# A streaming encoder layer: weight pool switched behind the third sample group, the attention's first work cast ahead, its scores queued in front of the memory values

## The chip, the core and the metric

The kernel runs on one core of one Trainium2 chip. The metric is the device time of one execution in microseconds (us); the time before is the median of three runs. The engines are TensorE (PE, matrix products into PSUM; its weight loads are shown as PEld), VectorE (DVE), ScalarE (ACT), GpSimd (POOL) and SyncE (SP, which only issues DMAs here). Each engine runs its own queue in order and waits on semaphores. DMAs are issued from the queues of SP and ACT before the change, and from POOL's too behind it; all run on the same sixteen DMA engines.

## What is computed

One layer with 1024 prompt tokens and 64 sample tokens, so 1088 columns, of width 1024, in float32. The change touches the sliding-window attention (SWA), the retention branch's output product and the memory values:

```python
def swa_attend(q, k, v, bias, sinks, valid):
    s = jnp.einsum('bnqhgd,bnkhd->bnhgqk', q, k, preferred_element_type=jnp.float32) * (SWA_HD ** -0.5)
    s = s + bias.astype(jnp.float32)
    if valid is not None:
        s = jnp.where(valid, s, NEG_INF)
    sink = sinks.astype(jnp.float32)[:, :, None, None]
    m = jnp.maximum(jnp.max(s, axis=-1, keepdims=True), sink)
    e = jnp.exp(s - m)
    p = e / (jnp.sum(e, axis=-1, keepdims=True) + jnp.exp(sink - m))
    return jnp.einsum('bnhgqk,bnkhd->bnqhgd', p.astype(v.dtype), v)

def merge_branches(ret_o, ret_g, swa_o, gate_a, gate_b, w_ret_out, w_swa_out, w_mix_out):
    B, S = ret_g.shape[:2]
    a = (rms_norm(ret_o).astype(ret_g.dtype).reshape(B, S, -1) * jax.nn.silu(ret_g)) @ w_ret_out
    b = swa_o.reshape(B, S, -1) @ w_swa_out
    return (jax.nn.sigmoid(gate_a) * a + jax.nn.sigmoid(gate_b) * b) @ w_mix_out

def mem_kv(mem, g_mem, w_mk, w_mv):
    B = mem.shape[0]
    mn = rms_norm(mem, g_mem)
    return ((mn @ w_mk).reshape(B, N_MEM, MEM_HEADS, MEM_HD),
            (mn @ w_mv).reshape(B, N_MEM, MEM_HEADS, MEM_HD))
```
Queries come in 17 chunks of 64 tokens; a chunk sees its own and the two chunks before it, so 192 keys, except chunk 0 (64 keys) and chunk 1 (128). There are 16 query heads of width 64 on two key heads.

## The kernel before

**Products.** Large products are made from two float32r parts of each operand, a high part (a cast on ACT, line 123) and the rest (a subtraction on DVE, line 124): high times high, high times low, low times high (lines 149 to 151, and 205 to 208 inside Strassen's scheme). A projection of 256 output rows is one round of Strassen with seven products, P1, P2, P6, P5, P7, P3 and P4 in PE's order. Its seven weight operands lie in tiles `wq` (five of them in rotation, `self.wbufs`), made from two `raw` tiles by sums on POOL (lines 183 to 189) and the two-part split. The pool `weights` that holds `raw` and `wq` is opened with five `wq` for `project_phase` and again, at the same place, with six for all that follows.

**project_phase.** It runs k, q, v and the sample groups of the attention's queries (`w_sq`, four groups, 0 to 3) between the four heads of retention, then `w_sk`/`w_sv` and the third sample group, then twelve projections in three sets of four: `w_ga`, `w_rg`, `w_gb`. Each set's results go through a `stage` tile to DRAM as `d_gate[1]`, `[0]`, `[2]`; the sets `w_ga` and `w_gb` are stored from ACT's queue, `w_rg` from SP's. `memory_phase` is a generator whose parts are drawn between these projections by the list `steps`; it makes memory keys and the values of three of the four heads, from weights in three `mw` tiles.

**mix_phase.** `swa` holds the attention's loop, `filler` the products that are strewn between its steps. Work is cut into 34 halves (17 chunks, two halves of the query heads). At step i PE gets, in this written order (`in_order` ties each to the last matmul): `weigh` of half i-1, `scores` of half i+2, `turn` of half i (transposes of the normalised weights), and some filler pieces; steps -2 and -1 only make scores. A half's `scores` go into one PSUM tile `s` of two banks that exists once; DVE adds the bias (line 958 or 961), takes the maximum (963), compares with the sink (964), negates (965); ACT takes the exponential (970, 972); DVE makes the reciprocal (973, 974), POOL multiplies (976). `turn` transposes keys 0 to 127 into `pt0`, copied by ACT (993), and keys 128 to 191 into `pt1` with four 64-row pieces side by side in 512 columns, copied by DVE (995). `weigh` multiplies them with the value tiles (1006): one pair of matmuls for each part, one for each key head, which write rows 0 to 63 and 64 to 127 of one PSUM bank.

The fillers are, in order: the loading and splitting of all 24 pieces of the retention operand (`d_gate[0]`, three column chunks `CH` of 384, 384 and 320 for eight row blocks, into tiles `ret` of ring 1), the fourth head's memory values (four pieces), and the 24 products with `w_ret_out` (row block m by column chunk c, two pieces of 12 matmuls each). Four pieces come at step -2, forty over the 34 steps, eight at the end.

**What sets the order.** A planner orders every engine's queue by a simulated time line; `high_priority` moves work ahead in it, and `issue_after(ins)` ties what follows behind `ins` on the same engine's queue without a wait for its end. A tile waits until the last reader of what lay at its address is done. The SBUF rings 0 and 1 have eight slots each: during the projections ring 0 holds the operands B11, T1 and T4 and two slots of `stage`, ring 1 B21, B22, T2 and T3; afterwards ring 0 becomes the attention's `swin` tiles (keys, queries, bias, values, and ten small load buffers `lds`), ring 1 the `ret` tiles. PSUM has eight banks: three pairs (`psa`) and two single ones (`pr`) in the projections; then three for the plain products (`pd`) and five for the attention (`pw`).

Of the kernel before, what the change touches and what calls it, by code (L numbers as in the profile page):

```python
# [19 lines left out]
P = 128  # L20
# [9 lines left out]
H = 4  # L30
# [79 lines left out]
class Kernel:  # L110
# [222 lines left out]
    def run(self):  # L333
        nc, tc, io = self.nc, self.tc, self.io
        with ExitStack() as ctx:
# [34 lines left out]
            with ExitStack() as sctx:  # L370
                self.rings = [Ring(sctx.enter_context(tc.tile_pool(name=f"ring{i}", bufs=1, reuse_waits="tile", side="right")))
                              for i in range(2)]
                self.mem = sctx.enter_context(ExitStack())
                with self.weights(5):
                    self.project_phase()
                with self.weights(6):
                    with self.plain_psum():
                        self.mix_phase()
                        self.mem.close()
                        self.cross_phase()  # L380
                    rp = sctx.enter_context(tc.tile_pool(name="rf", bufs=1, reuse_waits="tile", side="right"))
                    self.rstd_f = rp.tile([P, T], F32, name="rstd_f")
                    self.temp = sctx.enter_context(ExitStack())
                    self.new_b12(self.temp, side="right")
                    self.cross_out_phase()
                    self.ffn_phase()

    @contextmanager
    def weights(self, bufs):
        self.wbufs = bufs  # L390
        with ExitStack() as ctx:
            self.wp = ctx.enter_context(self.tc.tile_pool(name="weights", bufs=2, reuse_waits="tile"))
            yield
# [88 lines left out]
    def memory_phase(self, mp):  # L482
# [8 lines left out]
        room = lambda: mp.tile([P, 1024], F32, tag="mw", bufs=3, name="mw")  # L491
# [21 lines left out]
        for h in range(H - 1):  # L513
            us = [self.unit(io["w_mv"][h, i], 4, 256, room) for i in range(2)]
            for t in range(2):
# [10 lines left out]
    def bias_table(self):  # L526
# [11 lines left out]
        row = self.np.tile([1, 16], F32, tag="row", bufs=1, name="row")  # L538
# [3 lines left out]
        for e in range(2):  # L542
            rows = slice(e * 64, (e + 1) * 64)
            nc.vector.tensor_copy(self.sinks[rows, :], ps[rows, :16].rearrange("p (a b) -> p a b", b=2)[:, :, e])

    def project_phase(self):
        nc, tc, io = self.nc, self.tc, self.io
        with ExitStack() as ctx:
            self.fp = ctx.enter_context(tc.tile_pool(name="fa", bufs=1, reuse_waits="tile"))
# [84 lines left out]
            with ExitStack() as rctx:  # L634
# [4 lines left out]
                for h in range(H):  # L639
# [20 lines left out]
            project(self.load_ops((io["w_sk"], io["w_sv"])), lambda i, t, o: self.store(self.d_skv[i, :, half(t)], o))  # L660
            project(pair("w_sq", 3), queries(3))
            steps = [0, 0, 0, 0, 1, 2, 2, 3, 3, 3, 2, 0]
            for idx, w, act in ((1, "w_ga", AF.Sigmoid), (0, "w_rg", AF.Silu), (2, "w_gb", AF.Sigmoid)):
                for m in range(0, KT, 2):
                    store = nc.scalar.dma_start if idx else self.store
                    put = lambda i, t, o, idx=idx, m=m, store=store: store(self.d_gate[idx][m + i, :, half(t)], o)
                    other = None if idx else lambda i, m=m: self.d_ret[m + i]
                    with tc.issue_after(project(pair(w, m // 2), put, act, other)):
                        for i in range(steps.pop(0)):
# [3 lines left out]
                            else:  # L673
                                next(memory)

# [209 lines left out]
    def swa(self, ctx, fill):  # L885
        nc, tc, io = self.nc, self.tc, self.io
        if True:
# [4 lines left out]
            flat = [t.rearrange("p a b -> p (a b)") for t in self.ring_tiles(0, KT, "swin", F32)]  # L892
            kT, vT = flat[0][:, :KC], flat[5][:, :KC]
            bias = flat[2][:, :NPAIR * NKEY].rearrange("p (a b) -> p a b", b=NKEY)
            sinks = self.sinks
            qTs = [t[:, :16 * 2 * 64].rearrange("p (i c e) -> p i c e", i=4, c=4) for t in (flat[1], flat[7])]
            vts = [flat[4][:, i * P:(i + 1) * P] for i in range(17)] + [flat[0][:, KC + i * P:KC + (i + 1) * P] for i in range(3)]
            self.lds = [t[:, i * 384:(i + 1) * 384] for t in (flat[3], flat[6]) for i in range(5)]
            with tc.high_priority():
                def tokens(dst, i, cache):  # L900
                    self.load(dst[:, :SEQ], self.d_skv[i, :, :SEQ])
                    self.load(dst[:, SEQ:SEQ + P], io[cache])
                    self.load(dst[:, SEQ + P:], self.d_skv[i, :, SEQ:])

                tokens(kT, 0, "ckT")
                self.load_queries(qTs, 0)
                raws = [self.unit_raw(io["w_mv"][H - 1, i], 4, 256) for i in range(2)]
                self.first_units = [self.unit_parts(raw, 4, 256) for raw in raws]
            with tc.high_priority(), tc.issue_after(self.loaded):
                for e in range(2):  # L910
                    src = self.d_rb.rearrange("(p e) c -> e c p", e=2)[e, 63:63 + 64 * 255, :]
                    src = src.rearrange("(i c) p -> i p c", c=255)[:, :, :NKEY]
                    self.load(bias[e * 64:(e + 1) * 64], src)
# [26 lines left out]
            def scores(c, hf):  # L940
                ks, j0, nk = keys(c)
                if hf == 0 and c % 4 == 0 and c + 4 < 17:
                    self.load_queries(qTs, c + 4)
# [20 lines left out]
                nc.vector.tensor_tensor(out=nm, in0=nm, in1=snk, op=ALU.max)  # L964
                nc.vector.tensor_scalar(nm, nm, -1.0, None, ALU.mult)
                den = sw.tile([P, 2, 2], F32, tag="den", name="den")
                es = sw.tile([P, 2, 2], F32, tag="es", name="es")
                nc.vector.tensor_tensor(out=es, in0=snk, in1=nm, op=ALU.add)
# [3 lines left out]
                nc.scalar.activation(es, es, AF.Exp)  # L972
# [7 lines left out]
            def turn(c, hf):  # L980
                ks, j0, nk = keys(c)
                if hf == 0:
                    live[c] = [values(ks + k0) for k0 in range(0, nk, P)]
                t, vt = live.pop((c, hf)), live[c]
                parts = []
                for k0 in range(0, nk, P):
                    n = min(P, nk - k0)
                    pp = pw.tile([P, 512], F32, tag=f"pt{len(parts)}", name="pp")
                    for j, (v, i) in enumerate(units):
                        self.last_mm = nc.tensor.transpose(pp[:n, j * P:(j + 1) * P], t[:, v, i, k0:k0 + n], self.ident).ins  # L990
                    pT = sw.tile([P, 512], F32, tag=f"pT{len(parts)}", bufs=2, name="pT")
                    if len(parts) == 0:
                        nc.scalar.copy(pT[:n, :], pp[:n, :])
                    else:
                        nc.vector.tensor_copy(pT[:n, :], pp[:n, :])
                    parts.append((vt[k0 // P], pT, n))
                live[c, hf] = parts

            def weigh(c, hf):
# [4 lines left out]
                for j, (val, pT, n) in enumerate(parts):  # L1004
                    for v in range(2):
                        self.last_mm = mm(po[rows[v], hf * 256:(hf + 1) * 256], val[:n, rows[v]], pT[:n, v * 256:(v + 1) * 256],  # L1006
                                          start=j == 0, stop=j == len(parts) - 1).ins
# [13 lines left out]
            for i in range(-2, n):  # L1021
# [8 lines left out]
                if i == -2:  # L1030
                    with tc.high_priority(), tc.issue_after(self.operand_loaded):
                        tokens(vT, 1, "cvT")
                if i == 8:
                    with tc.issue_after(self.loaded):
                        keep()
            self.in_order(lambda: weigh(*halves[n - 1]))
            for pieces in next(fill):
                self.in_order(lambda: next(pieces, None))

# [19 lines left out]
    def filler(self):  # L1059

        nc, tc, io = self.nc, self.tc, self.io
        if True:
            def ld():
                self.lds.append(self.lds.pop(0))
                return self.lds[-1]

# [636 lines left out]
```

## Time and profile before

| | |
|---|---|
| median of three runs | 2243.72 us (2242.51 to 2244.74) |
| profiled execution, its own time | 2244.47 us |
| profiled execution, span from first to last instruction | 2242.7 us |
| mean granted PE clock | 0.988 |
| PE busy in 0 to 480 us | 458.36 us |
| PE busy in 1015 to 2242.7 us | 1190.29 us of 1227.70 |

The profile is one execution. Engine times are busy times; a group of instructions is given by its line, engine, operation and tiles, with its count, busy time, mean duration in ns and the idle time of its engine just ahead of it and what ended that. In a table of windows each row is a stretch of the span, with each engine's busy time, PE's granted clock as a share of full speed, and the DMA engines' busy share. In a timeline a row is start, duration, engine and line, with the count of merged instructions and in brackets the idle time ahead and what released it. Matmuls overlap in PE's pipeline, so their durations add up to more than the time that they take.

### The profile page before, as it was taken

How to read it: one execution, taken by the hardware profiler on the slowest of the kernel's cores; microseconds unless marked ns; L12 is line 12 of the kernel's file. 1: busy time of each engine (PE TensorE's matmuls, PEld its weight loads, DVE VectorE, ACT ScalarE, POOL GpSimd, SP SyncE). 2: the span in 40 equal slices, each digit the busy share in tenths (PEclk: the TensorE clock that was granted, in tenths of full speed). 3: DMA queues.
4: the chain of work that ended last, by engine and by line, in shares of the span. 5: the costliest groups of instructions: out<-in, count | busy, mean ns of one | idle time of the engine just before them, and what ended most of it. 6: DMA issues, size and time to landing. Idle time of an engine off the chain costs nothing.

```text
span 2242.7 us, 41756 instructions
## 1 busy us (share of the span) xinstructions
PE 2168.9 (97%) x16434; PEld 2105.3 (94%) x16434; DVE 1596.0 (71%) x2655; ACT 885.4 (39%) x1897; POOL 692.1 (31%) x466
## 2 busy tenths in 40 slices
PE   8899999999999989999999999999999999999986
PEld 8899999999999977779999998999999999999986
DVE  7986878666687667776455556668777677778587
ACT  7333333435444355554133333333323222344243
POOL 1441533342253112220000000014556555434462
PEclk9999999999999999999999999999999999999998
DMA  5533445443445475326443111422333332475233
GB/s 193 163 108 114 118 124 136 133 126 114 167 151 181 150 229 163 114 69 211 132 152 101 64 46 59 138 89 88 121 129 102 102 120 90 147 267 184 85 98 108
DMA packets 182599, 290.86 MB, mean 130 GB/s; under 512 B 40290, under 2 KB 110850, under 8 KB 182402
## 3 DMA queue, kind: packets, MB, share of 16 engines
q1 hardware_dynamic: 177794, 279.26, 39.3%
q10 hardware_dynamic: 4608, 8.91, 1.1%
q8 instruction: 130, 2.13, 0.4%
q14 instruction: 67, 0.55, 0.1%
HBM read 196.95 MB, written 91.16 MB: 128 GB/s over the span
## 4 chain that ended last, share of the span: by engine, by line
PE 79%; DVE 11%; DMA 5%; issue 2%; ACT 2%; POOL 1%; SPq 0%; DVEq 0%; ACTq 0%; POOLq 0%
PE pq L208 15%; PE pq L206 15%; PE pq L205 15%; PE pd L149 8%; PE pd L151 8%; PE pd L150 8%; DVE wq L124 2%; PE pout L1006 1%; DMA hl<-d_op 1%; PE pp L990 1%; PE pss L948 1%; DVE T L124 1%; DVE B L124 1%; DVE xg L1294 1%; DMA qs<-d_qkv 1%
## 5 line engine op out<-in xcount | busy, mean ns | idle before, releaser
L124 DVE TENSOR_TENSOR wq<-raw,wq 128x512 fp32r<-128x512 f32 (+1 forms) x505 | 448.8, 893 | 125.2 <-ACT wq L123 122.0
L123 ACT CAST wq<-raw 128x512 fp32r<-128x512 f32 (+1 forms) x505 | 307.5, 614 | 568.0 <-PE pq L208 259.1
L205 PE MATMUL pq<-T,wq 128*128 128x272 f32 x1832 | 492.9, 289 | 6.8 <-DVE u L252 3.6
L206 PE MATMUL pq<-T,wq 128*128 128x272 f32 x1832 | 493.0, 289 | 0.0
L206 PE MATMUL pq<-B,wq 128*128 128x272 f32 x1592 | 428.9, 289 | 9.1 <-DVE B L124 9.1
L205 PE MATMUL pq<-B,wq 128*128 128x272 f32 x1592 | 427.1, 289 | 0.2 <-ACT B L123 0.2
L208 PE MATMUL pq<-T,wq 128*128 128x272 f32 x1832 | 384.5, 290 | 3.4 <-DVE wq L124 3.4
L183 POOL TENSOR_TENSOR raw<-raw 128x512 f32<-128x512 f32 (+1 forms) x59 | 80.1, 1357 | 897.2 <-DVE rs_r L291 485.7
L205 PEld LDWEIGHTS pq<-T,wq 128*128 128x128 f32 x1832 | 346.1, 189 | 7.9 <-DVE u L252 3.7
L206 PEld LDWEIGHTS pq<-T,wq 128*128 128x128 f32 x1832 | 345.9, 189 | 0.3 <-issue 0.3
L208 PE MATMUL pq<-B,wq 128*128 128x272 f32 x1592 | 333.9, 290 | 0.0
L206 PEld LDWEIGHTS pq<-B,wq 128*128 128x128 f32 x1592 | 300.4, 189 | 11.0 <-DVE B L124 10.7
L205 PEld LDWEIGHTS pq<-B,wq 128*128 128x128 f32 x1592 | 300.2, 189 | 0.9 <-issue 0.4
L208 PEld LDWEIGHTS pq<-T,wq 128*128 128x128 f32 x1832 | 291.2, 190 | 4.6 <-DVE wq L124 3.8
L208 PEld LDWEIGHTS pq<-B,wq 128*128 128x128 f32 x1592 | 252.9, 190 | 0.5 <-issue 0.3
L252 DVE TENSOR_TENSOR u<-pq,u 128x544 f32<-128x544 f32 x177 | 127.6, 721 | 109.7 <-PE pq L208 109.2
L186 POOL TENSOR_TENSOR raw<-raw 128x512 f32<-128x512 f32 (+1 forms) x59 | 85.5, 1449 | 127.3 <-DVE wq L124 124.7
L976 POOL TENSOR_TENSOR t<-t,den 128x768 f32<-128x768 f32 (+2 forms) x34 | 47.9, 1408 | 170.7 <-DVE den L974 44.4
L571 DVE TENSOR_TENSOR stage<-pq,u 128x544 f32<-128x544 f32 x112 | 80.4, 718 | 26.4 <-PE pq L208 25.4
L184 POOL TENSOR_TENSOR raw<-raw 128x512 f32<-128x512 f32 (+1 forms) x59 | 87.3, 1480 | 3.7
L1461 POOL TENSOR_TENSOR y<-u,y 128x544 f32<-128x544 f32 x38 | 62.6, 1656 | 72.6 <-DVE y L1459 50.5
L189 POOL TENSOR_TENSOR raw<-raw 128x512 f32<-128x512 f32 (+1 forms) x59 | 83.3, 1412 | 4.4
(373 smaller groups left out, 4677.0 us busy)
## 6 DMA issues: line engine op xcount, KB each, us to landing
hl<-d_op SPq DMA_DIRECT2D x85, 272.0 KB, 4.6
d_qkv<-stage SPq DMA_DIRECT2D x44, 272.0 KB, 2.3
d_op<-stage SPq DMA_DIRECT2D x44, 272.0 KB, 2.4
d_op<-ht SPq DMA_DIRECT2D x44, 272.0 KB, 3.3
raw<-w_gate SPq DMA_DIRECT2D x22, 512.0 KB, 3.5
raw<-w_up SPq DMA_DIRECT2D x22, 512.0 KB, 3.6
d_gate<-stage ACTq DMA_DIRECT2D x32, 272.0 KB, 2.7
raw<-w_down SPq DMA_DIRECT2D x16, 512.0 KB, 4.2
```

The lines of the kernel that those rows point to most:

```text
L123: self.last_cast = self.nc.scalar.copy(hi, src).ins
L124: return self.nc.vector.tensor_tensor(out=lo, in0=src, in1=hi.bitcast(F32), op=ALU.subtract).ins
L149: mm(ps, wh, xh, start=start, stop=False)
L150: mm(ps, wh, xl, start=False, stop=False)
L151: self.last_mm = mm(ps, wl, xh, start=False, stop=stop).ins
L184: tt(out=a21, in0=a21, in1=a22, op=add)
L186: tt(out=a11, in0=a22, in1=a11, op=sub)
L189: tt(out=a12, in0=a12, in1=a11, op=sub)
L205: mm(ps[:, c, :HC], w[:, 0, ks], x[:, 0, cs], start=start, stop=False)
L206: mm(ps[:, c, :HC], w[:, 0, ks], x[:, 1, cs], start=False, stop=False)
L208: self.last_mm = mm(ps[:, c, :HC], w[:, 1, ks], x[:, 0, c * HC:(c + 1) * HC], start=False, stop=stop).ins
L252: add = lambda out, a, b: nc.vector.tensor_tensor(out=out, in0=a, in1=b, op=ALU.add)
```

## The change

The `weights` pool is no longer a context of its own. It is closed and opened again with six `wq` inside `project_phase`, right behind `w_sk`/`w_sv` and the third sample group, with the Strassen sums' pool `fa` opened again above it; `mw` goes from three tiles to two. The plain products' PSUM pool moves to the other side. `memory_phase` gets one more part at its end, which loads and splits the weights of the fourth head's values. `begin_swa`, called at the end of `project_phase`, loads keys, the first queries and the bias, and `first_loads` the first chunk of the retention operand and the first `w_ret_out` unit, with their high parts cast on ACT; the low parts follow on DVE behind the first two halves' maxima. The second and third chunk are loaded and split inside the loop. The four fillers of step -2 move to step -1, behind both first scores, and become six; 38 are left for the 34 steps. The first two row blocks of `w_ret_out` run chunk by chunk. The stores of the last `w_gb` projection and of the fourth head's values go from ACT's and SP's queues to POOL's. A second query load moves from step -2 to step 2.

In the loop, a table `minus` of negative sinks makes maximum and negation one step. Keys 128 to 191 are transposed so that the second key head's land in rows 64 to 127 of the PSUM tile (from a 128-key piece that begins at key 64), the copy is 128 by 256 instead of 64 by 512, and the second head's matmul reads rows 64 to 127 of the copy and of a value tile that begins 64 keys earlier; one such tile more is needed in all.

```diff
-                with self.weights(5):
-                    self.project_phase()
-                with self.weights(6):
-                    with self.plain_psum():
+                self.weights(5)
+                self.project_phase()
+                with self.plain_psum(side="right"):
...
-        room = lambda: mp.tile([P, 1024], F32, tag="mw", bufs=3, name="mw")
+        room = lambda: mp.tile([P, 1024], F32, tag="mw", bufs=2, name="mw")
...
+            project(self.load_ops((io["w_sk"], io["w_sv"])), lambda i, t, o: self.store(self.d_skv[i, :, half(t)], o))
+            project(pair("w_sq", 3), queries(3))
+            fctx.close()
+            self.weights(6)
+            self.sums_pool(ctx)
...
-                    store = nc.scalar.dma_start if idx else self.store
+                    store = nc.gpsimd.dma_start if (idx, m) == (2, KT - 2) else nc.scalar.dma_start if idx else self.store
...
+            next(memory)
+            self.begin_swa()
...
-                yield [pieces] * 4
                 yield []
-                count, steps, done = 48 - 8, 2 * 17, 0
+                yield [pieces] * 6
+                count, steps, done = 48 - 10, 2 * 17, 0
...
-                nc.vector.tensor_tensor(out=nm, in0=nm, in1=snk, op=ALU.max)
-                nc.vector.tensor_scalar(nm, nm, -1.0, None, ALU.mult)
+                nc.vector.scalar_tensor_tensor(nm, nm, -1.0, quad(self.minus), ALU.mult, ALU.min)
...
+                if nk == NKEY:
+                    pp = pw.tile([P, 512], F32, tag="pt1", name="pp")
+                    for v, i in reversed(units):
+                        k0, n = (64, P) if v else (P, 64)
+                        self.last_mm = nc.tensor.transpose(pp[:n, i * P:(i + 1) * P], t[:, v, i, k0:k0 + n], self.ident).ins
+                    pT = sw.tile([P, 256], F32, tag="pT1", bufs=2, name="pT")
+                    nc.vector.tensor_copy(pT, pp[:, :256])
+                    parts.append([(vt[2 - v][rows[v]], pT[rows[v]]) for v in range(2)])
...
+        self.rets = [self.rings[1].tile(f"ret{k}", slot=i) for k, i in enumerate((0, 1, 4, 5, 6, 7, 2, 3))]
+        self.marks = []
+        self.first_loads()
...
+    def first_loads(self):
+
+        nc, (c0, n) = self.nc, CH[0]
+        after, self.first = self.loaded, []
+        raw = self.unit_raw(self.io["w_ret_out"][0], KT)
+        for k in range(KT):
+            a = self.ld()[:, :n]
+            with self.tc.issue_after(after):
+                self.last_operand = self.load(a, self.d_gate[0][k, :, c0:c0 + n])
+            r = self.rets[k][:, :, c0:c0 + n]
+            self.first.append((a, r[:, 0], r[:, 1]))
+            nc.scalar.copy(r[:, 0], a)
+        qs = [self.new_op() for i in range(2)]
+        for i, q in enumerate(qs):
+            a = raw[:, i * 512:(i + 1) * 512]
+            nc.scalar.copy(q[:, 0], a)
+            self.first.insert(i * 5, (a, q[:, 0], q[:, 1]))
...
+    def first_low(self):
+
+        with self.tc.issue_after(self.marks[-1][0]):
+            for a, hi, lo in self.first:
+                self.nc.vector.tensor_tensor(out=lo, in0=a, in1=hi.bitcast(F32), op=ALU.subtract)
+
+    def later_operands(self, c0, n, ks):
+
+        a, b = self.marks[-1]
+        with self.tc.issue_after(a), self.tc.issue_after(b):
+            for k in ks:
+                x = self.ld()[:, :n]
+                with self.tc.issue_after(self.last_operand):
+                    self.last_operand = self.load(x, self.d_gate[0][k, :, c0:c0 + n])
+                self.split(x, self.rets[k][:, 0, c0:c0 + n], self.rets[k][:, 1, c0:c0 + n])
...
+            order = [(m, c) for c in range(3) for m in range(2)] + [(m, c) for m in range(2, KT) for c in range(3)]
+            halves = [range(4), range(4, KT)]
+            extra = {2: (1, 0), 3: (1, 1), 5: (2, 0), 7: (2, 1)}
```

More of the change, by code (lines that the diff above doesn't have):

```diff
@@ L544, in bias_table @@
             nc.vector.tensor_copy(self.sinks[rows, :], ps[rows, :16].rearrange("p (a b) -> p a b", b=2)[:, :, e])
+        self.minus = self.np.tile([P, 16], F32, tag="row", bufs=1, name="minus")[:, :NPAIR]
+        nc.vector.tensor_scalar(self.minus, self.sinks, -1.0, None, ALU.mult)
     def project_phase(self):
@@ L890, in swa @@
             mm = nc.tensor.matmul
[L892 to L896, printed above, removed]
-            vts = [flat[4][:, i * P:(i + 1) * P] for i in range(17)] + [flat[0][:, KC + i * P:KC + (i + 1) * P] for i in range(3)]
[L898 to L913, printed above, removed]
+            flat, kT, bias, qTs, sinks = self.flat, self.kT, self.bias, self.qTs, self.sinks
+            vT = flat[5][:, :KC]
+            vts = [flat[4][:, i * P:(i + 1) * P] for i in range(17)] + [flat[0][:, KC + i * P:KC + (i + 1) * P] for i in range(3)]
             def keep():
@@ L1062, in filler @@
         if True:
-            def ld():
-                self.lds.append(self.lds.pop(0))
-                return self.lds[-1]
-            rets = self.ring_tiles(1, KT, "ret")
-            def operands(c0, n):
-                after = self.loaded
-                for k in range(KT):
-                    a = ld()
-                    with tc.issue_after(after):
-                        ins = self.load(a[:, :n], self.d_gate[0][k, :, c0:c0 + n])
-                    if c0 == 0:
-                        self.operand_loaded = ins
-                    self.split(a[:, :n], rets[k][:, 0, c0:c0 + n], rets[k][:, 1, c0:c0 + n])
-            for c0, n in CH:
-                operands(c0, n)
+            ld, rets = self.ld, self.rets
+            self.first_low()
             us, h = self.first_units, H - 1
```

139 lines of the change are left out of this document (85 added, 54 removed).

## The prediction

> **What bounds the kernel now.** I read the page's span and engine totals, then a table of windows by stage, then the hand-over stage in windows of 5 us, then its timeline and waits, and last the groups of the attention loop.
>
> ```profile
> span 2242.7 us, 41756 instructions
> PE 2168.9 (97%) x16434; PEld 2105.3 (94%) x16434; DVE 1596.0 (71%) x2655; ACT 885.4 (39%) x1897; POOL 692.1 (31%) x466
> ```
> ```profile
> core 0: us, PE busy (x) PEld busy (x) DVE busy (x) ACT busy (x) POOL busy (x), PEclk, DMA share, GB/s
> 480.00:815.00 335.00, 335.00 (x2708) 333.10 (x2707) 234.43 (x357) 148.85 (x268) 100.51 (x68) 1.00 0.48 153
> 815.00:860.00 45.00, 30.60 (x185) 25.20 (x183) 33.44 (x83) 30.93 (x98) 5.30 (x5) 0.81 0.81 267
> 860.00:1015.00 155.00, 154.61 (x1103) 119.96 (x1102) 124.24 (x270) 81.50 (x311) 41.22 (x29) 1.00 0.32 99
> ```
> TensorE (PE) is busy for 2168.9 of 2242.7 us. In the projections (480 to 815) it never rests, and in the loop of the sliding-window attention (860 to 1015) it rests for 0.4 us. Between them lies the hand-over, 45 us with 30.60 of PE: 14.40 us idle, at a granted clock of 0.81. This is the stage that the change rewrites; what it takes away elsewhere has to be worth PE time to count.
>
> ```profile
> 815.00:820.00 5.00, 2.17 (x17) 1.52 (x15) 2.18 (x4) 2.19 (x5) 0.00 (x0) 0.93 0.49 150
> 820.00:825.00 5.00, 4.99 (x32) 4.99 (x33) 4.30 (x12) 4.91 (x15) 0.00 (x0) 0.73 0.82 245
> 825.00:830.00 5.00, 3.98 (x39) 3.35 (x37) 4.58 (x15) 3.01 (x11) 0.77 (x1) 1.00 1.04 385
> 830.00:835.00 5.00, 0.26 (x1) 0.07 (x1) 4.07 (x13) 4.94 (x21) 1.35 (x2) 0.80 1.01 361
> 835.00:840.00 5.00, 3.42 (x11) 3.20 (x12) 4.81 (x8) 3.82 (x8) 0.60 (x1) 0.52 0.76 245
> 850.00:855.00 5.00, 2.28 (x17) 1.61 (x17) 2.86 (x8) 2.52 (x12) 1.07 (x1) 0.85 0.91 265
> 855.00:860.00 5.00, 5.00 (x18) 3.96 (x16) 2.02 (x7) 2.63 (x11) 1.50 (x1) 0.50 0.34 123
> 860.00:865.00 5.00, 5.00 (x39) 3.76 (x37) 4.36 (x9) 1.88 (x6) 0.91 (x1) 0.97 0.73 216
> ```
> Idle time is 5 minus the PE column: 2.83 us in the first window, 4.74 in 830:835, 2.72 in 850:855. The clock column hides a second loss. A mean of 0.73 over 5 us is 2.7 us at half speed (0.27 x 5 x 2). So counted, half speed lasts 3.4 us in 815:825, 6.8 in 830:840 and 6.8 in 850:865. PE's work there takes twice its time; the loss is half of the busy part: 3.4 / 2 = 1.7; half of the 0.26 + 3.42 busy in 830:840, less a little at the end that ran at full speed, 1.6; half of about 6.1, 3.0. Together 6.3 us. **The hand-over loses 14.4 + 6.3 = 20.7 us**, the most that the change can win there.
>
> The timeline names the three waits:
>
> ```profile
> 815.97 0.72 DVE L571 TENSOR_TENSOR stage<-pq,u 128x544 f32<-128x544 f32 x1 [1.50 <-PE pq L208]
> 816.73 0.72 DVE L577 TENSOR_TENSOR stage<-stage,rstd 128x544 f32<-128x544 f32 x1
> 816.74 0.66 PE L948 MATMUL pss<-swin,swin 64*128 64x64 f32 x8 [0.82 <-DVE stage L571]
> 818.62 2.18 ACT L123 CAST wq<-raw 128x512 fp32r<-128x512 f32 x4 [0.48 <-ACT stage L580]
> 819.29 0.58 PE L149 MATMUL pd<-wq,ms 128*128 128x256 f32 x1 [1.88 <-ACT wq L123]
> 826.97 0.66 PE L948 MATMUL pss<-swin,swin 64*128 64x64 f32 x8
> 827.72 0.48 DVE L961 SCALAR_TENSOR_TENSOR t<-pss,swin 128x128 f32<-128x128 f32 x2
> 828.34 0.72 PE L948 MATMUL pss<-swin,swin 64*128 64x128 f32 x8 [0.71 <-DVE t L961]
> 836.58 0.69 PE L149 MATMUL pd<-ret,wq 128*128 128x384 f32 x1 [6.32 <-ACT wq L123]
> 854.22 1.11 PE L990 MATMUL pp<-ident,t 128*128 128x128 f32 x4 [2.15 <-POOL t L976]
> ```
> ```profile
> 808.96 12.44 SPq L117 DMA_DIRECT2D swin<-d_gate  x7
> SPq L117 <- DMA d_gate<-stage: 11.6, 4, 5.6
> raw<-w_ret_out SPq DMA_DIRECT2D x5, 512.0 KB, 6.0
> ```
> The last projection's product ends at about 815.9; the first scores wait 0.82 us for its PSUM to be drained, the memory values wait for casts that ACT begins only behind its last activation, the first product of `w_ret_out` waits 6.32 us for a weight that was cast at 835.9, and the first 192-key transposes wait for a softmax whose Vector (DVE) and ACT steps lay behind casts. Behind the casts stand loads: SP took 12.44 us to issue seven gate loads, and 11.6 us of SP's waits were for stores of the last gate group from ACT's queue, which share no data with them. From 825 to 835 the DMA engines were then full.
>
> **The change, part by part.**
>
> *Casts and loads ahead; the last group's gate stores and the last memory values' stores from POOL's queue.* With the pool switched earlier, the memory values' weights (four casts), the first eight retention operands and the first `w_ret_out` unit are loaded and half cast while the last products still run. DVE is busy 234.43 of 335 and ACT 148.85 in the projections, so there is room. The 11.6 us of SP waits go with the four stores that caused them, and only eight operand loads (192 KB each) instead of 24 come before the first product; 16 move into the loop, where the DMA share is 0.32. So the 6.32 us wait and most of the 2.83 go. An issue from POOL's queue is not in this trace; the nearest rows are an issue from ACT's and POOL's idle time:
>
> ```profile
> 818.17 0.35 ACTq L666 DMA_DIRECT2D d_gate<-stage  x1
> 826.61 0.77 POOL L976 TENSOR_TENSOR t<-t,den 128x256 f32<-128x256 f32 x1 [28.82 <-ACT ret L123]
> ```
> POOL rests for 28.82 us ahead of its first normalisation, so I take 0; bounds 0 and 2.8 us (eight issues of 0.35), the latter only if all come ahead of that normalisation and the transposes wait. The Trainium skill, DMA: Bandwidth & Descriptors, specifications, puts a POOL-queue DMA's first byte at about 1 us against 0.6 from the others; no run here shows it yet, and by an estimate from it eight take 8 us of POOL, still inside its idle time.
>
> *Scores in front of values.* The PSUM pool moves to the other side, so the first scores no longer wait for the last drain (0.82 gained). The second scores need the first's bank back, freed by DVE: by the rows at 826.97 to 828.34 a gap of 0.71 us if DVE is free, plus up to 2 x 0.72 if it finishes the projection's last two steps first. I take 1.4 (bounds 0.7 and 2.1).
>
> *DVE becomes the close engine.* Its work from 816 to the loop's fifth step, from these rows:
>
> ```profile
> L124 DVE TENSOR_TENSOR ret<-swin,ret 128x384 fp32r<-128x384 f32 x16 | 9.9, 645 | 1.4 <-ACT ret L123 1.3
> L124 DVE TENSOR_TENSOR wq<-raw,wq 128x512 fp32r<-128x512 f32 x10 | 6.5, 688 | 2.4 <-ACT wq L123 2.2
> L965 DVE TENSOR_SCALAR nm<-nm 128x4 f32<-128x4 f32 x6 | 1.0, 168 | 0.1
> 847.60 0.33 PE L151 MATMUL pd<-ret,wq 128*128 128x384 f32 x1
> 847.77 0.34 PE L149 MATMUL pd<-ret,wq 128*128 128x384 f32 x1
> ```
> It was 33.4 us before; four weight casts (4 x 0.69) go ahead and six small steps (6 x 0.17) are fused away: about 29.7. PE's own work there is 45 - 20.7 = 24.3 us, plus two filler pieces that now come before the loop (12 matmuls each, started 0.17 us apart: 4.1), 28.4. DVE is 1.3 us over even if it never waited. Two steps of lead in the loop absorb part. I take 2.0 us of PE waiting, bounds 0 and 6.
>
> *Later operands inside the loop.* Each group of four has one load to land (6.0 us for a large one in the busy stage), four casts and four DVE steps, 6.0 + 4 x 0.65 plus ACT's, some 10 us, and it is asked for two steps of the loop before its use. The loop passes 28 steps (the x28 of the next fence) in its 155 us, 5.5 each, the first ones with fewer keys less: 8 to 11 us. I take 1.0; bounds 0 and 5.
>
> *Clock.* The three gaps, each of 2.7 us or more, brought half-speed spells of 3.4 or 6.8 us. Those that I leave are shorter; I take one spell of 3.4: 1.7 lost; bounds 0 and 3.4.
>
> *Pool switch at the third sample group.* New tiles wait for the old ones at their address; the first new weight may wait for the group's last product and then be cast. PE was never idle there, so any wait is a loss: 0 if retention work fills it, up to 2.0 (a cast on ACT, one on DVE, hand-offs). I take 0.5. One room less for the memory weights: sixteen units come in the last two thirds of the projections' 335 us, some 14 us apart, against 6.0 for a load, so 0; where units come in a row that cover is gone, at up to 6.0 us each.
>
> *Negative table, packed copy.*
>
> ```profile
> L964 DVE TENSOR_TENSOR nm<-nm,sinks 128x4 f32<-128x4 f32 x28 | 7.5, 269 | 0.5
> L965 DVE TENSOR_SCALAR nm<-nm 128x4 f32<-128x4 f32 x28 | 7.6, 272 | 0.9
> L995 DVE COPY pT<-pp 64x512 f32<-64x512 f32 x29 | 19.6, 676 | 0.5 <-PE pp L990 0.3
> 914.44 0.19 PEld L1006 LDWEIGHTS pout<-pT,swin 64*64 64x64 f32 x4 [0.38 <-issue]
> 915.02 0.92 PE L948 MATMUL pss<-swin,swin 64*128 64x192 f32 x8
> L1006 PE MATMUL pout<-pT,swin 64*64 64x256 f32 x112 | 18.2, 402 | 0.0
> ```
> Each half saves one of two small steps (0.27) and up to half of a 0.68 copy: at most 0.6 us of DVE. DVE is not what PE waits for in the loop (0.4 us idle in 155), so 0. The transposes stay eight a half; one more value transpose in all, 0.2. The matmuls of the last keys keep their count, but one of each pair moves to rows 64 to 127. Four of mean 402 ns now fit in 0.58 us (914.44 to 915.02), so the pair runs side by side. I take 0 for the move.
>
> **Sum:** 20.7 - 1.4 - 2.0 - 1.0 - 1.7 - 0.5 - 0.2 = 13.9 us. From the profiled execution's 2244.47 (1.8 beyond its span) that is 2230.6. It stood 0.75 above the median of 2243.72, so I forecast **2230**.
>
> **Rivals.**
>
> *A: the packed pair no longer runs side by side (slower).* Both matmuls now read different halves of the rows but write one PSUM bank; before, the pair shared the rows. The scores' pairs, which also split the rows, write two banks, so no row here shows this form. If they go one after the other, a half costs another 0.58, and if each waits for the end of the one before, 4 x 0.40 - 0.58 = 1.03. Thirty halves have 192 keys: 17.4 to 31 us, middle 24, giving 2230.6 + 24 = 2255. It makes the change slower beyond noise from (13.9 + 4.5) / 30 = 0.61 us a half. Against it: the outputs lie in different partitions. The Trainium skill, TensorEngine Tiling (Array Packing), Restrictions and Gotchas, says that different row tiles cannot access the same PSUM bank at once; by that rule A happens, by the 0.58 row alone it does not.
>
> *B: DVE and the late operands eat half.* The bounds 6 and 5 in place of 2.0 and 1.0, less what they share: some 8 us won less, 2238. For it: 33.4 us of DVE in 45. Against: two steps of lead.
>
> *C: the first work isn't ahead.* Instruction order is a planner's; if the casts stay behind ACT's last activation or SP's loads behind other waits, the idle 2.83, part of the 6.32 and their half-speed spells stay: about 11 us, so 2241.6. For it: before, the casts stood there too. Against: the stores that blocked SP have left.
>
> **How the numbers follow.** Forecast 0.60, A 0.13, B 0.17, C 0.10. Runs of this kernel spread by 0.1%, so 0.2% (4.5 us) is about what can be told from no change: faster means below 2239.2. Faster: 0.58 of the forecast's, 0.11 of B, 0.03 of C: 0.72. Slower: A nearly whole and 0.01 of C: 0.13. Same: 0.15. The forecast's own range is 2224 (all terms at their small ends leave 18 to 20 us won) to 2238; taking in C it is 2224 to 2243, with A left out.
>
> **What would show it.** Right: between the last product and the first 192-key transposes PE idles under 6 us; the first `w_ret_out` matmul waits under 1; SP no longer waits for gate stores; from 480 to the hand-over PE stays full; the loop keeps 0.58 us for the last keys' four matmuls. Wrong: this 0.58 above 1.1 (A); PE waiting on DVE for several us behind the hand-over (B); ACT's first casts behind its last activation (C); or a new PE gap near 500.

## The result, and the profile after

The changed kernel takes 2255.68 us (median of 6 runs, 2254.49 to 2262.11) against 2243.45 us for the kernel before on the same chip (6 runs, 2238.34 to 2244.79): a ratio of 1.0062, 95% interval 1.0046 to 1.0077. It is 12.2 us slower, where 2230 was forecast. The profiled execution took 2257.46 us with a span of 2255.7.

The totals of the page, and windows by stage of the changed kernel. Its last projection product ends at 842.4 and not at 815.9, so the last two windows begin there and are about as long as the pair of before that follows. The columns behind the length of a window are the busy times of PE, PEld, DVE, ACT and POOL, then PE's clock, the DMA share and GB/s.

```profile
span 2255.7 us, 41727 instructions
PE 2179.8 (97%) x16435; PEld 2111.8 (94%) x16435; DVE 1576.1 (70%) x2622; ACT 878.5 (39%) x1892; POOL 691.3 (31%) x474
```
```profile
480.00:815.00 335.00, 320.86 (x2496) 314.56 (x2495) 219.67 (x340) 135.05 (x249) 90.96 (x65) 0.96 0.43 138
...
842.40:907.40 65.00, 58.57 (x403) 47.15 (x405) 51.82 (x120) 42.02 (x149) 16.71 (x17) 0.95 0.70 220
907.40:1042.00 134.60, 134.60 (x954) 104.31 (x953) 88.66 (x201) 68.04 (x256) 35.78 (x24) 1.00 0.29 89
```
The same stretches of the kernel before:

```profile
815.00:880.00 65.00, 50.60 (x330) 41.14 (x328) 50.19 (x118) 41.07 (x134) 11.18 (x9) 0.87 0.73 235
880.00:1015.00 135.00, 134.61 (x958) 104.02 (x958) 107.50 (x236) 71.36 (x274) 35.34 (x25) 1.00 0.28 89
```
The hand-over is better, as forecast: 6.4 us idle instead of 14.4, the clock 0.95 instead of 0.87. The loss is in the projections from 480 to 815, where PE never rested before: 14.1 us idle, clock 0.96. In windows of 5 us it lies behind the pool switch:

```profile
505.00:510.00 5.00, 2.29 (x18) 2.07 (x17) 3.37 (x10) 2.21 (x5) 2.53 (x2) 0.97 0.60 148
510.00:515.00 5.00, 4.04 (x19) 3.64 (x18) 3.67 (x7) 2.65 (x6) 1.84 (x3) 0.50 0.92 296
515.00:520.00 5.00, 5.00 (x38) 5.00 (x37) 2.87 (x4) 2.48 (x5) 3.72 (x3) 0.85 0.09 31
...
530.00:535.00 5.00, 1.48 (x8) 1.08 (x8) 3.22 (x8) 2.10 (x5) 0.78 (x1) 0.86 0.00 0
535.00:540.00 5.00, 4.26 (x18) 3.86 (x19) 2.40 (x6) 1.42 (x3) 0.00 (x0) 0.50 0.21 66
...
545.00:550.00 5.00, 2.29 (x9) 1.37 (x10) 2.34 (x10) 1.80 (x6) 0.00 (x0) 0.72 0.19 52
550.00:555.00 5.00, 5.00 (x14) 2.58 (x14) 1.27 (x6) 1.04 (x4) 0.00 (x0) 0.50 0.15 52
555.00:560.00 5.00, 3.35 (x14) 2.70 (x13) 3.24 (x8) 2.47 (x4) 0.00 (x0) 0.50 0.33 85
```
PE's waits from 505 to 560, and lines of the timeline there (start, duration, instruction, the idle time before it), then two of the kernel before:

```profile
PE pb L843 <- ACT ret_o L839: 11.6, 4, 3.9
PE pk L713 <- DVE ret_t L845: 1.9, 2, 1.0
```
```profile
507.21 1.07 SPq L117 DMA_DIRECT2D raw<-w_ga  x2
...
511.56 1.14 ACT L123 CAST wq<-raw 128x512 fp32r<-128x512 f32 x2 [0.33 <-DMA raw<-w_ga]
...
528.65 0.41 PE L208 MATMUL pq<-T,wq 128*128 128x272 f32 x2
...
556.53 0.51 ACT L839 ACTIVATE ret_o<-ret_o,rr 64x256 f32<-64x256 f32 x1 [1.90 <-DVE rr L298]
556.94 0.59 ACT L255 COPY u<-pq 128x544 f32<-128x544 f32 x1
```
```profile
483.24 4.60 SPq L117 DMA_DIRECT2D raw<-w_ga  x2
...
511.30 0.60 ACT L255 COPY u<-pq 128x544 f32<-128x544 f32 x1
```
Lines 833 to 845 are the end of a retention step, a chain of small ACT and DVE steps. In the kernel before, PE ran products of the next group between its links. Now there are none to run. The load of the first `w_ga` weights is issued at 507.21 (before: 483.24), so PE has no product to run from the last one of `w_sq` until the weights are cast at 512. Then `w_ga` gets as far as its third product, ending at 529: three products fill the three pairs of PSUM banks, and the first `u` copy that would empty one is executed on ACT only at 556.94, directly behind ACT's last retention step and without a wait of its own: it stands there in ACT's queue. Before, it stood between retention steps at 511.30. From 529 to 557 PE has only the retention's own chain.

In the hand-over, PE's waits by releaser, changed kernel from 842 to 1038 (the list of before had 8.2 us for `wq`, 2.5 for POOL's normalisation, 2.1 for ACT's copy):

```profile
PE pout L1004 <- ACT pT L985: 3.6, 2, 2.1
PE pss L944 <- DVE t L957: 1.7, 2, 1.5
PE pout L1004 <- DVE pT L993: 0.8, 1, 0.8
PE pd L150 <- DVE ret L1091: 0.2, 1, 0.2
```

### The profile page after: what moved, and what is told of

Same layout as the page of the kernel before. It is cut to its first block, busy times and chain, and to the rows that moved or that the text cites. A ratio compares the mean times of both kernels' runs of the same rounds, so it can differ in the third digit from the quotient of the medians.

```text
span 2255.7 us, 41727 instructions
## 1 busy us (share of the span) xinstructions
PE 2179.8 (97%) x16435; PEld 2111.8 (94%) x16435; DVE 1576.1 (70%) x2622; ACT 878.5 (39%) x1892; POOL 691.3 (31%) x474
## 4 chain that ended last, share of the span: by engine, by line
PE 76%; DVE 12%; DMA 4%; ACT 3%; issue 2%; POOL 2%; SPq 0%; DVEq 0%; ACTq 0%; POOLq 0%
PE pq L208 14%; PE pq L205 14%; PE pq L206 14%; PE pd L149 7%; PE pd L151 7%; PE pd L150 7%; DVE wq L124 2%; PE pout L1004 1%; DMA hl<-d_op 1%; PE pss L944 1%; DMA qs<-d_qkv 1%; DVE B L124 1%; DVE stage L580 1%; DVE xg L1352 1%; DVE T L124 1%
```

## The experiments

Three questions were open. Is the hole at 505 to 560 the switch itself, or what the new layout does, or the early casts and loads? What is the rest of the change worth without it? And do the loop's edits cost nothing and gain nothing?

A fact of the layout matters for the first. The left side of memory is one stack: two load tiles, the operand buffers (4096 bytes of a partition each), the four sums u1, u2, u3, u5 (2176 each), then the retention's pool. With a sixth operand buffer the new sums lie 4096 bytes higher, and the upper two (u3 and u5) reach into what was the retention's pool; u1, the first to be written, doesn't.

**1. `before_with_switch`: the switch alone, put into the kernel before**, as in the changed kernel (one weight pool of five up to there, two rooms for the memory's weights).

```
+            fctx.close()
+            self.weights(6)
+            self.sums_pool(ctx)
-        room = lambda: mp.tile([P, 1024], F32, tag="mw", bufs=3, name="mw")
+        room = lambda: mp.tile([P, 1024], F32, tag="mw", bufs=2, name="mw")
```


> The kernel before with the early pool switch alone (six operand buffers behind the third sample group, sums lifted by 4 KB, one room less for the memory's weights); hand-over and loop as before. Reach theory: the hole near 510 comes in, about 24 us: 2267 (2262 to 2272), hand-over unchanged with 14 to 15 us of PE idle. Other-edit theory (early casts make the hole): no change, 2243.

Measured: 2262.41 us, before 2241.83; ratio 1.0087 (1.0065 to 1.0108). The loss is 20.6 us with nothing else of the change in the kernel, and from 480 to 815 PE idles 14.4 us here too. The early casts and loads are not its cause. The other half of the expectation missed: the hand-over did not stay as it was. Its waits, from the last product on, come to 9.7 us instead of 14.6, and the 6.3 us for the first `w_ret_out` weight are not among them:

```profile
PE pss L954 <- DVE stage L574: 4.3, 1, 4.3
PE pp L996 <- POOL t L982: 4.2, 2, 3.8
PE pss L954 <- DVE es L974: 1.2, 1, 1.2
```
From the last product's end (841.74) to the start of the loop's last values (1041.19) this kernel takes 199.4 us, the one before 206.4 (815.93 to 1022.28). So the switch alone delays the last product by 25.8 us and wins 6.9 us behind it.

**2 and 3. `gap_into_retention` and `gap_inside_sums`: how far the sums move.** In both, the switch stays where it is, with five operand buffers, and an empty tile of 512 bytes lifts the sums. In the second the old sums' pool is also 512 bytes larger, so that the lifted sums stay inside it.

```
-            self.weights(6)
+            self.weights(5)
+            gp = ctx.enter_context(tc.tile_pool(name="gp", bufs=1, ...))
+            gp.tile([P, 128], F32, name="gap")
             (only gap_inside_sums, ahead of fctx.close():)
+            self.fp.tile([P, 128], F32, name="gap2")
```


> The changed kernel, but the new weight pool has five operand buffers like the old one, and a gap of only 512 bytes lifts the sums' tiles. The third row of operands' sixth buffer is gone, so nothing of the weights moves. Reach theory: any reach into the retention's addresses is enough, even 512 bytes under the last sums' tile, so the hole between 505 and 565 stays: 2255 (2250 to 2261). Switch theory: about the same, 2255. If the sixth operand buffer, which lies where the first two sums were, is what waits: 2231.

> As the run before, five buffers and the sums lifted by 512 bytes, but the old sums' pool is 512 bytes larger, so that the lifted tiles stay inside it and share no address with the retention. Reach theory: the hole is gone, PE full between 505 and 565, 2231 (2227 to 2238, five operand buffers instead of six may cost the later stages a little). Switch theory: 2255, since the pools are switched at the same place and every sums' tile lies across two old ones.

Measured: 2257.76 us (ratio 1.0071, 1.0045 to 1.0097) and 2236.73 us (0.9971, 0.9960 to 0.9982). Windows of the first and its first `u` copy of `w_ga` in the timeline, then the same of the second:

```profile
505.00:520.00 15.00, 11.18 (x71) 10.60 (x70) 9.94 (x20) 6.86 (x16) 8.29 (x6) 0.77 0.55 159
520.00:565.00 45.00, 34.31 (x208) 30.31 (x208) 20.72 (x54) 15.78 (x38) 2.86 (x2) 0.81 0.36 112
```
```profile
555.40 0.59 ACT L255 COPY u<-pq 128x544 f32<-128x544 f32 x1
```
```profile
505.00:520.00 15.00, 11.33 (x71) 10.71 (x70) 9.76 (x20) 6.69 (x14) 7.98 (x6) 0.77 0.54 157
520.00:565.00 45.00, 45.00 (x369) 44.78 (x368) 31.34 (x64) 26.65 (x49) 8.48 (x6) 1.00 0.37 118
```
```profile
522.26 0.60 ACT L255 COPY u<-pq 128x544 f32<-128x544 f32 x1
```
A reach of 512 bytes under the last sum holds back even u1, which shares no byte with the retention: its copy comes at 555.40 behind the whole retention instead of 522.26. Why it is placed there, though it shares nothing, no run shows. This is the larger cause, 2257.76 - 2236.73 = 21 us. The sixth buffer as such is not in either kernel. From 505 to 520 both are alike and both lose: 3.7 us idle at a clock of 0.77. That is a second cause, and it belongs to the switch itself.

**4. `late_switch`: the same switch behind the four `w_ga` groups**, when the retention is over: the block from `fctx.close()` to `memory = ...` moved into the loop, ahead of the first `w_rg` group.

> The changed kernel with one edit: the weight and sums pools are closed and opened anew behind the four groups of w_ga, when the last retention head is over, and not behind the third sample group. Reach theory (the new sums' tiles lie 4 KB higher and reach into the retention's addresses, so the first sums stand behind the last retention work; PE loses 14.0 us idle and some 10.6 us at half clock between 505 and 565): PE is full again there, the u copy of the first w_ga group stands between retention steps, the time falls by about 24 us to 2231 (2227 to 2236). Switch theory (closing and opening the weight pool stalls wherever it is put): the loss moves behind w_ga's groups, the time stays 2250 or more. Other-edit theory (the early casts and loads take the engines from retention): the loss near 510 stays, 2250 or more.

Measured: 2239.57 us (0.9988, 0.9977 to 1.0000). The time lies between what the reach theory and the switch theory gave, and each was partly right. 505 to 560 is full again, but PE now stands at the new place, where it waits 3.33 us for the first `w_rg` cast. This is the switch's own loss, moved:

```profile
605.00:610.00 5.00, 3.85 (x31) 3.63 (x30) 2.56 (x5) 1.32 (x2) 0.00 (x0) 1.00 0.30 111
610.00:615.00 5.00, 2.81 (x14) 2.81 (x15) 1.67 (x3) 2.17 (x4) 1.93 (x2) 0.78 0.14 56
615.00:620.00 5.00, 5.00 (x38) 5.00 (x37) 2.67 (x3) 2.35 (x6) 3.53 (x3) 0.88 0.01 3
```
The idle time and, by the two clocks, some 1.7 us of half clock make 5 us. That does not cover the whole distance to the kernel without a switch (experiment 6, 7.6 us lower in another session); the rest is open.

**5. `switch_loads_kept`: what the switch itself costs.** `gap_inside_sums` with the two load tiles in a pool of their own that stays open.

```
-            raw = self.wp.tile([P, 1024], F32, tag="raw", bufs=2, name="raw")
+            raw = self.raws.tile([P, 1024], F32, tag="raw", bufs=2, name="raw")
```


> As gap_inside_sums (pools switched at the third sample group, five buffers, no reach into the retention), but the two tiles that weights are loaded into have a pool of their own that is never closed. Theory: of the switch's some 6 us most comes from the load of the first w_ga weights, issued at 507 and not at 483 since the new tile stands behind the whole old pool; with the load early again only a cast on ACT and one on DVE are left of it, PE idles 2 us or less near 507: 2232 to 2234. Rival (the operand tiles' wait is enough): the hole stays 3.7 us with its half clock, 2237.

Measured: 2230.29 us (0.9938, 0.9924 to 0.9951), 6.4 us below `gap_inside_sums` and a little below what was expected. The two ran in different sessions; by their ratios to the kernel before the distance is 7.4 us. The load is issued at 483.21 again and the wait that is left is a cast's, 1.13 us, with no half clock behind it:

```profile
505.00:520.00 15.00, 13.58 (x109) 13.14 (x108) 13.56 (x22) 9.02 (x17) 8.34 (x6) 1.00 0.35 94
```
```profile
507.17 0.39 PE L205 MATMUL pq<-B,wq 128*128 128x272 f32 x1 [1.13 <-ACT wq L123]
```
So the switch's own price was in the main the load's 24 us of lead, which the load tiles lose when their pool is closed; the operands' wait for a free buffer is at most what is left here.

**6. `no_switch`: the rest of the change alone.** The three lines from `fctx.close()` to `self.sums_pool(ctx)` are left out; five buffers to the end.

> The changed kernel without any pool switch: one weight pool of five operand buffers and one sums' pool from the first projection to the end; all other edits as they are. Theory: of the 24 us lost after 500 the reach cost 18 and the switch itself 6 (new operand and raw tiles wait for the whole old pool: in the last run that kept the switch PE idled 3.7 us and ran 6 to 7 us at half clock between 505 and 520). Without a switch both go: PE full from 400 to the last product, 2230 (2226 to 2234). If the 6 us came from another edit of the change, they stay: 2236.

Measured: 2231.95 us, before 2241.51; 0.9947 (0.9931 to 0.9963). PE is full from 480 to 815. But the second scores wait longer than in the changed kernel, behind DVE, which waits for a cast; the guess of experiment 7 is that this cast needs a free operand buffer:

```profile
819.17 0.69 DVE L124 TENSOR_TENSOR wq<-mw,wq 128x512 fp32r<-128x512 f32 x1 [4.23 <-ACT wq L123]
...
821.80 1.12 PE L941 MATMUL pss<-swin,swin 64*128 64x64 f32 x8 [4.80 <-DVE t L954]
```
**7. `sixth_buffer`: six buffers without a switch.** Every sixth operand comes from a pool of one tile on the right side of memory, opened when the retention is over and given up behind `mix_phase`. From there on this kernel has five, where the kernel before and the changed one have six.

```
+        if self.sixth is not None and self.count_op % 6 == 0:
+            return self.sixth.tile([P, 2, 512], F32R, tag="wq6", bufs=1, name="wq")
...
+                if idx == 0:
+                    self.sixth = self.mem.enter_context(tc.tile_pool(name="wq6", ..., side="right"))
...
+                    self.sixth = None
```


> As no_switch, with the sixth operand buffer as a tile of its own, opened at the first w_rg group on the other side of memory, so that nothing is moved or closed. In no_switch the fourth cast of the last memory values waits for a free operand buffer, DVE drains the last product behind it, and the second scores wait 4.80 us; with six buffers in the changed kernel it was 1.47. Theory: this gap is about 1.5 again, the half-clock spell behind it goes too, 3 to 5 us below no_switch: 2228 (2225 to 2230). Rival (the bias rows' load is what is late): the gap stays, 2232.

Measured: 2230.04 us, before 2243.68; 0.9934 (0.9921 to 0.9946). The gap is 1.48 us again. Against `no_switch` the ratio falls by 0.0013 with overlapping intervals: the gap is settled, its worth in time is not.

**8 and 9. The second `w_ret_out` unit loaded earlier**, without and with the sixth buffer.

```
+        with self.tc.issue_after(self.last_operand):
+            self.second = self.unit_raw(self.io["w_ret_out"][1], KT)
...
-                units = {0: self.first_out, 1: self.unit(io["w_ret_out"][1], KT)}
+                units = {0: self.first_out, 1: self.unit_parts(self.second, KT)}
```


> As no_switch, and the second w_ret_out unit is loaded behind the first eight retention operands and not behind the memory values' last scaling. In the changed kernel ACT's copy of the first transposed weights stood behind a cast that waited 7.13 us for this load; PE idled 2.14 us and then ran at half clock. Theory: that gap goes, 2 to 5 us below no_switch, 2226 to 2228. Rival: the load only takes the DMA engines from the key and value loads and another wait takes its place: within 1.5 us of no_switch.

> Sixth buffer as in sixth_buffer, and the second w_ret_out unit loaded behind the first retention operands as in no_switch_early_unit. Theory: the 2.14 us that PE waits for ACT's copy (ACT stands at a cast that waits 7.13 us for this unit's load) go too: 1 to 3 us below sixth_buffer, 2226 (2222 to 2229). Rival: loads for the values' keys come later instead, no gain.

Measured: 2230.36 us (0.9948, 0.9930 to 0.9965) and 2228.85 us, before 2243.68 (0.9929, 0.9915 to 0.9943). Neither can be told from its parent, as the rival has it. With the sixth buffer PE still waits for ACT's copy, as much as without the early load (2.7 us there):

```profile
PE pout L1008 <- ACT pT L989: 3.3, 2, 2.2
```
`sixth_early_unit` has the lowest median of all, though its interval overlaps that of four others. It beats both kernels: its ratio to the kernel before is 0.9929, the changed kernel's 1.0062.

**10. `no_switch_gates_on_act`: the last gate group's stores back on ACT's queue.**

> As no_switch, but the last gate group's stores are issued from ACT's queue again and not from POOL's. Theory of the prediction: SP's loads wait for those stores again (4 waits, up to 11.6 us of SP before the change), the first operands and the first w_ret_out product come later: 2 to 6 us above no_switch. Rival: the loads were moved ahead by the early first work, the queue of the stores is of no account: within 1.5 us of no_switch.

Measured: 2232.81 us (0.9958, 0.9944 to 0.9971), the rival's number. SP's waits for gate stores don't come back either; its longest waits between 800 and 885 are for DVE and for `d_mix` stores. So no effect of the stores' queue can be told; that it is the early first work that moved the loads fits this, but was not tested alone.

**11. `no_switch_old_loop`: old last-key code and the two old small steps.**

> As no_switch, but the loop has the old last-key code (two copies of 512 columns, pairs of matmuls on the same rows) and the old two small steps for the negative maximum. Prediction: the packed pair and the fused step are worth nothing to PE, within 2 us of no_switch. Packed-pair rival: undoing it wins 17 us or more. DVE rival: DVE has 0.27 + 0.26 us a half more to do, and PE waits on it behind the hand-over: 2 to 6 us above no_switch.

Measured: 2236.41 us (0.9970, 0.9955 to 0.9984), 4.5 above `no_switch`, though the intervals overlap a little; from the start of the first scores to that of the loop's last values it takes 202.9 us in place of 198.1. So the packed-pair rival falls, and the DVE rival fits. In windows of the loop from 880 to 1015 DVE works 107.62 us with the old code and 90.82 with the new. With the old code PE waits for DVE's copy and POOL's normalisation (between 815 and 1015):

```profile
PE pss L941 <- DVE t L954: 4.1, 2, 3.8
PE pp L983 <- POOL t L969: 2.7, 5, 1.1
PE pout L999 <- DVE pT L988: 2.2, 1, 2.2
```
## Why the prediction was wrong

**The step that failed** is the one named "pool switch at the third sample group", 0.5 us with bounds 0 and 2.0. It measured some 27 us: 21 for the reach into the retention (experiments 2 and 3) and 6.4 for the switch itself (3 and 5). The changed kernel's trace agrees: its last product ends at 842.38 instead of 815.93, 26.5 us later. Of the signs named beforehand it is the last, a new PE gap near 500. The step failed twice.

First, it took the wait to be one between a new tile and the old tile at its address, and looked at the operands alone. It did not set the new sums' addresses, 4096 bytes higher, against the retention's, whose last head still runs beside `w_ga`. And its cover, "0 if retention work fills it", ran the wrong way: retention steps leave holes that projection products fill. Without the products the holes are bare, which is the 11.6 us of waits for `ret_o`.

Second, the step's upper bound was a cast on each engine and the hand-offs. The row that would have given it is the load's: it was issued at 483.24 in the kernel before, 24 us ahead of where the switch put it, and this lead belonged to the closed pool too. With the lead kept the bound held: 1.42 us idle in experiment 5.

**The rest of the sum came near its total, in part by luck.** Without its 0.5 it said 14.4 us won. `sixth_buffer` has all other edits, six buffers up to the end of the attention and no switch, and wins 13.6. The two causes less this gain, 27.4 - 13.6 = 13.8, come near the 12.2 measured. But the sum speaks of the hand-over and the loop alone. The loop's last values begin, in the kernel before, the changed kernel and `sixth_buffer`, at:

```profile
1022.28 1.23 PE L1006 MATMUL pout<-pT,swin 128*64 128x256 f32 x8
```
```profile
1037.56 1.23 PE L1004 MATMUL pout<-pT,swin 128*64 128x256 f32 x8
```
```profile
1013.68 1.23 PE L1008 MATMUL pout<-pT,swin 128*64 128x256 f32 x8
```
From the last product's end (815.93, 842.38, 817.90) that is 206.4, 195.2 and 195.8 us: 11.2 and 10.6 won there, not 14.4. Behind the loop the profiled execution of the changed kernel is another 2.3 us shorter than before and that of `sixth_buffer` 5.8, for which the sum has no term; what they are due to is open.

By terms: the wait of 6.32 us for the first `w_ret_out` weight went and PE's first product of it follows the memory values at once; the score gap was put at 1.4 and measured 1.47. The idle terms were 1.4, 2.0 and 1.0, together 4.4, and PE idled 6.4; half clock was put at 1.7, and a clock of 0.95 over 65 us costs some 3.2. PE idles 5.5 us between the last product and the first 192-key transposes at 879.96 (under 6 was promised). The loop kept its time for the last keys' four matmuls, from the changed kernel's timeline:

```profile
926.53 0.20 PEld L1004 LDWEIGHTS pout<-pT,swin 128*64 128x64 f32 x4 [0.25 <-issue]
...
927.11 0.20 PEld L1004 LDWEIGHTS pout<-pT,swin 64*64 64x64 f32 x4 [0.38 <-issue]
...
927.69 0.63 PEld L944 LDWEIGHTS pss<-swin,swin 64*128 64x128 f32 x8 [0.39 <-issue]
```
0.58 us from the second line to the third, as before (914.44 to 915.02). So rival A is dead, although its 2255 is the time that was measured: the right number by luck, for a wrong reason. The rule of the Trainium skill, TensorEngine Tiling (Array Packing), Restrictions and Gotchas, that different row tiles cannot access one PSUM bank at once, would have made it more than 1.1; this trace doesn't agree where the outputs lie in different partitions. Rivals B and C did not happen: PE waited 2.7 us for DVE in the whole stretch, and ACT's first operand casts began at 839.98, ahead of its last activation.

**Two reasons were wrong without harm.** The gate stores' change of queue was credited with SP's 11.6 us; experiment 10 shows nothing for it beyond the noise. The packed copy and the fused step were costed at 0, since DVE rests in the loop; they are worth about 4.5 us in experiment 11, where PE waits longer for DVE's copy and POOL's normalisation with the old code; the likely reason is that in the loop's first steps DVE has late casts as well and is the close engine there. The prediction had said so under "DVE becomes the close engine" and had already taken the six fused steps off DVE's sum.

## What to carry to other kernels

Before a pool is closed and opened anew in the middle of work, write down for each new tile which old pools lie at its address, and when the last instruction of each runs, not only of the tile with the same name; here 512 bytes of reach under the last tile held back the first one too. Ask the same of the load tiles, because what a switch takes first is the lead of the next load. And where PE is full only because one stage's products fill another's waits, holding back either stage costs the sum of those waits, with the half clock behind them.

## What the runs showed of the hardware

A wait of the same length was followed by the half clock in one run and not in others. In the changed kernel the second scores waited 1.47 us and the clock of the two windows around it (840 to 850) was 1.00; in `sixth_early_unit` they waited 1.48 us and the clock from 815 to 825 was 1.00; in `sixth_buffer` they waited 1.48 us at the same place of the program:

```profile
815.00:820.00 5.00, 3.52 (x34) 3.27 (x32) 3.36 (x7) 4.95 (x11) 0.55 (x1) 1.00 0.77 240
820.00:825.00 5.00, 5.00 (x33) 4.93 (x34) 2.11 (x11) 4.66 (x15) 1.15 (x3) 0.68 0.70 248
```
The windows of 505 to 560 above show 0.50 as the lower clock, so 0.68 over 5 us is 3.2 us at half speed. The price of such a gap was thus its own length in two runs, and that and some 1.6 us more in the third; a sum over gaps near 1.5 us should carry both.

A store issued on POOL's queue took 0.54 us of POOL where the one on ACT's queue had taken 0.35 (818.17 in the kernel before):

```profile
845.73 0.54 POOL L678 DMA_DIRECT2D d_gate<-stage  x1 [1.74 <-ACT stage L589]
```
The prediction's upper bound of 2.8 us for eight such issues went by ACT's row; at 0.54 each they take 4.3. Here it did no harm: POOL still rested 3.59 us ahead of its first normalisation at 850.94.
